# Five edits to a two-layer transformer kernel: a gate's transpose placed later, 384-column halves in two places, a scaling tied to another instruction, and probabilities times values for two key blocks in a row

## The chip, the cores and the metric

The kernel runs on one core of a Trainium2 chip, in one launch. The metric is the device time of that launch in microseconds (us); the time before is the median of three runs. The profile shows one execution. Its engines: PE is TensorE (PEld its weight loads), DVE is VectorE, ACT is ScalarE, POOL is GpSimd, SP is SyncE, which issues the DMAs here. All arrays are fp32, or fp32r where a matmul reads the high or the low part of a split number.

## The reference

Two layers of width 1024 over 512 latent tokens and 256 context tokens. Layer 0 has windowed grouped-query attention (16 heads of 64, 2 key heads, windows of three 128-blocks plus the context, a sink logit per head), layer 1 differential attention (8 heads with two score maps each). Each is followed by a squared-ReLU MLP of width 4096; a conditioning vector gives six modulation vectors per layer (`mod_x`), two of them gates.

```python
for i in range(DEPTH):
    mod_x = silu(c) @ w_ada[i] + b_ada[i]
    sh1, sc1, g1, sh2, sc2, g2 = split(mod_x)
    hx = x * (1 + sc1) + sh1
    ax = window_gqa(hx, hc, ...) if i % 2 == 0 else diff_attention(hx, hc, ...)
    x = layer_norm(alpha * x + g1 * ax, ln1_g[i], ln1_b[i])
    fx = square(relu((x * (1 + sc2) + sh2) @ mlp_w1[i])) @ mlp_w2[i]
    x = layer_norm(alpha * x + g2 * fx, ln2_g[i], ln2_b[i])
    # in layer 0 the context tokens go the same way, with their own modulation
```

In window_gqa, for a block of 128 queries: `p = softmax_with_sink(s)`, `o = p[:, lat] @ v + p[:, ctx] @ vc`.

## The kernel before

PE's instructions stand in an order that the program itself plans: `Flow` is a small simulation with jobs (generators) of given priorities; a job yields a condition, and the first job whose condition holds goes on and appends its matmuls. Costs such as `mm(n)`, `dve(n)` and `act(n)` are the planner's. The other engines and the DMA queue are ordered by the framework's scheduler; each engine then works in its order.

Every large product is made of three matmuls (`mm3`, L318 to L320): high x high, high x low, low x high. A weight tile of 128x1024 comes by DMA (w_raw), is rounded by ACT to w_h (`wsplit`), and DVE subtracts for w_l; the DMAs stand in SP's queue at L275.

Layer 0, attention (`group`, L957): 24 jobs, one for each of 6 token blocks and 4 groups of four heads. Scores go to s_ps (L977, L981), DVE and ACT make the probabilities e, then for each key block in turn four PE transposes fill pT_ps (L1028), ACT or DVE in turn copies it to pT, and `av` multiplies by the values into o_ps (L1014; one call gives four records of 128x256, in two column halves). Token blocks 0 to 5 have 4, 5, 5, 4, 2 and 2 key blocks. `pend` holds blocks whose transposes are out; a block's product is put in as soon as its own copy is done by the planner's time.

Layer 0, MLP (`mlp`, L641): four chunks of 1024 hidden units, each an up projection of 8 weight tiles over all 768 tokens (h_ps, tokens as columns in two parts, 512 and 256), squared ReLU (`post`), and a down projection of twelve groups (y_ps, weights as columns). In chunk 0 two of the tiles go in pieces of 256 columns, which leaves 30 tiles in two parts. Beside chunk 0 and later ones, the rows of the modulation (`ada_rows`, products with w_adaT on DVE into mods) are worked off as a filler. When the rows of (0, 5), the gate of this MLP, are complete, `ada_gate` starts at priority 0: `to_rows` has PE transpose mods into gate_t (L435), ACT copy it to gate_s, and a DMA write gate_d (L441). `g2` reads it at chunk 2.

Layer 1, attention: per head `proj1` makes qkv_ps for six token blocks, `post1` splits and ropes them (sk, sq, vt) and transposes to kT_ps (L1229) and qT_ps; `scores1` makes 8 score tiles per head of 128x768 in s_ps (L1324: 512 and 256 columns), whose minimum DVE takes and whose exponential ACT; `att1` transposes and multiplies. Beside it `resid1` computes the scaled residual in 16 pieces on POOL, each released (`behind`) by a kT transpose of heads 1 to 4 and blocks 0 to 3; for every four pieces it loads a part of the layer norm's gain and bias (rs_g, rs_b), which DVE scales by ALPHA (the operation is recorded at L260).

Of the kernel before, what the change touches and what calls it, by code (L numbers as in the profile page):

```python
# [19 lines left out]
P = 128  # L20
# [214 lines left out]
def hybrid_block(ctx: ExitStack, tc: tile.TileContext, t: dict, out: bass.AP):  # L235
# [27 lines left out]
    def ac(n, deps, fn, lat=LAT, **kw):  # L263
        fn(**kw)  # L264
        return fl.op("A", act(n), deps, lat)
# [176 lines left out]

    def ada_gate(l, m, dep):
        gd = dram.tile([2 - l, KT, P], F32, name=f"gate_d{l}{m}")
        yield from to_rows(mods[l][:, m] if l == 0 else mods[l][:, m, :, 0], gd, dep)
        gate_d[(l, m)] = gd.rearrange("s k p -> s (k p)")

# [193 lines left out]
    def mlp(l, hx, ready, apool, pool, ntok, acc, gates, done, extra, res, XR=0):  # L641
        ntb = ntok // P
        first = [slice(i, i + 256) for i in range(0, ntok, 256)]
        parts = [slice(0, 512)] + ([slice(512, ntok)] if ntok > 512 else [])
        fx = [pool.tile([P, D], F32, name="fx", tag="fx", bufs=ntb) for _ in range(ntb)]


# [16 lines left out]

        row_gates = gates
        for ch in range(4):
            hid = [apool.tile([P, 2, 2, ntok], F32R, name="hid", tag="A", bufs=4) for _ in range(4)]
            state = {}

            def post(ft, pt, slot, p):  # L670
                hd, fi = hid[ft // 2], ft % 2
                r = pool.tile([P, max(ntok, XR)], F32, name="relu", tag="xr", bufs=2)
                a = ac(ntok, [p], nc.scalar.activation, out=r[:, :ntok], in_=pt[:, :ntok], func=AF.Relu)
                if slot is not None:
                    sS.give(slot, a)
                if ch:
                    a = gp(pool2(ntok), [a], nc.gpsimd.tensor_tensor, out=r[:, :ntok], in0=r[:, :ntok],
                           in1=r[:, :ntok], op=ALU.mult)
                else:
                    a = dv(ntok, [a], nc.vector.tensor_tensor, out=r[:, :ntok], in0=r[:, :ntok], in1=r[:, :ntok],  # L680
                           op=ALU.mult)
                split(ntok, a, r[:, :ntok], hd[:, fi, 0], hd[:, fi, 1])
# [3 lines left out]
            for n, (ft, sl) in enumerate(order):  # L686
# [11 lines left out]
                yield w.t  # L698
                for k in range(KT):
                    c_ = slice(k * P, (k + 1) * P)  # L700
                    mm3(pt[:, sl], w.h[:, c_], w.l[:, c_], hxs(hx, k, 0, sl), hxs(hx, k, 1, sl), k == 0, k == KT - 1)
                    if k % 4 == 3:
                        p = fl.pe(12 * mm(sl.stop - sl.start))
                        if k == 3:
                            yield
# [21 lines left out]
    with tc.tile_pool(name="qpool", bufs=6, side="right") as qpool, \  # L727
# [229 lines left out]
        def group(n, tb, qd):  # L957
# [60 lines left out]
                return p  # L1018


            i = 0
            while i < len(kbs) or pend:
                yield lambda: (YES if (i < len(kbs) and fl.ok([sm_.ok, pS.ok])) or (pend and fl.ok(pend[0][3])) else NO)
                if i < len(kbs) and fl.ok([sm_.ok, pS.ok]) and len(pend) < 4:
                    pp = psm("pT_ps")
                    slot = sm_.take()
# [12 lines left out]
                    pend.append((i, kbs[i], pt_, r, xi))  # L1039
                    i += 1  # L1040
                else:
                    p = av(*pend.pop(0))
            st0["done"] += 1
            if st0["done"] % 4 == 0:
                eS.free += [p] * (1 if st0["done"] == 4 else 2)
# [132 lines left out]
    with tc.tile_pool(name="attn1", bufs=1, reuse_waits="tile") as pool:  # L1178
# [104 lines left out]
        def resid1():  # L1283
            def load(n):
                i, tb = n // NXB, n % NXB
                c = slice(i * 256, i * 256 + 256)
                if tb == 0:
                    gb[:] = [pool.tile([P, 256], F32, name="rs_" + n_, tag="rs_" + n_, bufs=1) for n_ in "gb"]
                    for k in range(2):
                        dma(256, [], out=gb[k], in_=lnrow[0, 2 + k:3 + k][:, c].broadcast_to([P, 256]))  # L1290
                        dv(128, [], nc.vector.tensor_scalar, out=gb[k], in0=gb[k], scalar1=ALPHA, scalar2=None,
                           op0=ALU.mult)
                x = pool.tile([P, 256], F32, name="rs_x", tag="rs_x", bufs=3)
                return x, dma(256, [], out=x, in_=x_spill[tb][:, c]), x_res[tb][:, c], list(gb)

# [2 lines left out]
            for n in range(4 * NXB):  # L1298
                after = yield
                x, q, dst, (g, b) = nxt  # L1300
                d = gp(pool2(256), [q], behind(nc.gpsimd.tensor_tensor, after), out=x, in0=x, in1=g, op=ALU.mult)
                d = gp(pool2(256), [d], nc.gpsimd.tensor_tensor, out=x, in0=x, in1=b, op=ALU.add)
                if old:
# [8 lines left out]
        def scores1(hd_, R):  # L1312
            kS, qTt = R["kS"], R["qT"]
            yield lambda: R["ready"]
            for qb in range(4):
                em = []
                for tt in range(2):
# [1 line left out]
                    ei = eS1.take()  # L1319
                    sp = psS("s_ps")  # L1320
                    slot = sS.take()
                    for c0, c1 in ((0, 512), (512, TOK)):
                        for hl in range(2):
                            nc.tensor.matmul(out=sp[:, c0:c1], lhsT=qTt[:, tt, hl, qb * P:(qb + 1) * P],  # L1324
                                             rhs=kS[:, tt, c0:c1], start=(hl == 0), stop=(hl == 1))
                    p = fl.pe(2 * mm(512) + 2 * mm(256))
                    nm = small.tile([P, 1], F32, name="nm", tag="nm")
                    d = dv(TOK, [p], nc.vector.tensor_reduce, out=nm, in_=sp[:, 0:TOK], axis=AX.X, op=ALU.min)
                    e = pool.tile([P, TOK], F32, name="e1", tag="e", bufs=EB1)
                    if tt == 0:  # L1330
                        sm = st["s0"][hd_ // NG][:, qb, hd_ % NG:hd_ % NG + 1]
                    else:
                        sm = small.tile([P, 1], F32, name="sm", tag="sm")
                    a = ac(TOK + 200, [d], nc.scalar.activation, out=e, in_=sp[:, 0:TOK], func=AF.Exp, scale=-1.0,
                           bias=nm, accum_out=sm)
                    sS.give(slot, a)
                    em.append((e, sm, ei, a))
                    yield
# [290 lines left out]
```

## Time and profile before

| | |
|---|---|
| median of three runs | 1710.75 us (1710.18 to 1711.88) |
| the profiled execution, its own time | 1715.99 us |
| its span, first to last instruction | 1714.2 us |
| mean granted clock of PE | 0.985 |
| PE busy | 1634.3 us, 95% |
| DVE, ACT, POOL busy | 957.7, 658.1, 345.9 us |

The profile's times are from one execution and count from its first instruction. A matmul's record ends with its last result, so consecutive ones overlap, and the distance of their starts is what one costs. The granted clock of a stretch is a share of 2.4 GHz; 0.5 is 1.2 GHz, and the two levels are the only ones seen.

### The profile page before, as it was taken

What the parts mean: (1) busy time and instruction counts of PE and PEld (TensorE: products, weight loads), DVE (VectorE), ACT (ScalarE), POOL (GpSimd) and SP (SyncE); (2) the same over time, 40 slices, a digit from 0 to 9 for tenths busy, and PEclk for the clock granted to TensorE, in tenths of its full rate; (3) what the DMA queues carried; (4) which work ended last, traced back from release to release, by engine and by line L of the source; (5) the groups of instructions that cost most, each with busy time, mean ns of one, the idle gap of its engine ahead of it and who ended that gap; (6) DMA issues with size and microseconds to landing.
All of it is one profiled execution on the core that took longest, in us unless ns stands there. A gap on an engine that the chain in (4) does not pass through costs nothing.

```text
span 1714.2 us, 23438 instructions
## 1 busy us (share of the span) xinstructions
PE 1634.3 (95%) x9129; PEld 1359.1 (79%) x9129; DVE 957.7 (56%) x1811; ACT 658.1 (38%) x1281; POOL 345.9 (20%) x314
## 2 busy tenths in 40 slices
PE   6899899999899999999999999999989799999998
PEld 4787567788778878878878998999877788888886
DVE  3665677676764644445346767777655553233336
ACT  3455555462212302302315555555542533223230
POOL 1233444200001201243220122220100001103422
PEclk9999999999999999999999999999999899999999
DMA  9110441243443434324222222211132214232321
GB/s 361 40 50 32 148 171 52 84 169 112 159 147 111 148 111 141 111 91 156 81 81 102 63 68 66 72 44 37 47 111 99 99 62 134 74 121 76 111 86 50
DMA packets 57240, 174.78 MB, mean 102 GB/s; under 512 B 7144, under 2 KB 13096, under 8 KB 57128
## 3 DMA queue, kind: packets, MB, share of 16 engines
q1 hardware_dynamic: 57128, 173.27, 29.9%
q8 instruction: 72, 1.18, 0.3%
q14 instruction: 40, 0.33, 0.1%
HBM read 165.35 MB, written 7.90 MB: 101 GB/s over the span
## 4 chain that ended last, share of the span: by engine, by line
PE 75%; DVE 9%; issue 5%; ACT 4%; POOL 3%; DMA 3%; SPq 0%; POOLq 0%; DVEq 0%; ACTq 0%
PE y_ps L320 10%; PE y_ps L319 10%; PE y_ps L318 10%; PE h_ps L318 8%; PE h_ps L319 8%; PE h_ps L320 8%; PE o_ps L1014 2%; PE qkv_ps L318 2%; PE s_ps L1324 2%; PE qkv_ps L319 2%; PE qkv_ps L320 2%; DVE e L260 2%; DVE w_l L260 2%; PE pT_ps L1028 2%; ACT w_h L264 1%
## 5 line engine op out<-in xcount | busy, mean ns | idle before, releaser
L264 ACT CAST w_h<-w_raw 128x1024 fp32r<-128x1024 f32 (+1 forms) x185 | 186.5, 1014 | 425.5 <-PE y_ps L320 214.1
L260 DVE TENSOR_TENSOR w_l<-w_raw,w_h 128x1024 fp32r<-128x1024 f32 (+1 forms) x185 | 221.9, 1209 | 223.5 <-ACT w_h L264 223.4
L319 PE MATMUL y_ps<-w_l,hid 128*128 128x512 f32 x640 | 253.0, 395 | 2.2 <-DVE w_l L260 2.2
L320 PE MATMUL y_ps<-w_h,hid 128*128 128x512 f32 x640 | 252.9, 395 | 0.6 <-DVE hid L260 0.6
L318 PE MATMUL y_ps<-w_h,hid 128*128 128x512 f32 x640 | 253.0, 395 | 0.0
L268 POOL TENSOR_TENSOR relu<-relu 128x768 f32<-128x768 f32 (+1 forms) x48 | 81.5, 1697 | 613.9 <-ACT relu L264 613.9
L320 PE MATMUL h_ps<-hx0m,w_l 128*128 128x256 f32 (+1 forms) x528 | 176.2, 334 | 0.9 <-DVE w_l L260 0.9
L318 PE MATMUL h_ps<-hx0m,w_h 128*128 128x256 f32 (+1 forms) x528 | 176.7, 335 | 0.0
L319 PE MATMUL h_ps<-hx0m,w_h 128*128 128x256 f32 (+1 forms) x528 | 176.0, 333 | 0.0
L319 PEld LDWEIGHTS y_ps<-w_l,hid 128*128 128x128 f32 x640 | 120.4, 188 | 31.7 <-DVE w_l L260 3.9
L320 PEld LDWEIGHTS y_ps<-w_h,hid 128*128 128x128 f32 x640 | 120.4, 188 | 30.1 <-DVE hid L260 1.9
L318 PEld LDWEIGHTS y_ps<-w_h,hid 128*128 128x128 f32 x640 | 120.4, 188 | 28.4
L318 PE MATMUL qkv_ps<-w_h,hx 128*128 128x384 f32 (+1 forms) x384 | 128.2, 334 | 0.2
L319 PE MATMUL qkv_ps<-w_l,hx 128*128 128x384 f32 (+1 forms) x384 | 123.7, 322 | 0.8 <-DVE w_l L260 0.8
L320 PE MATMUL qkv_ps<-w_h,hx 128*128 128x384 f32 (+1 forms) x384 | 123.4, 321 | 0.0
L268 POOL TENSOR_TENSOR e<-e,sm 128x512 f32<-128x512 f32 (+2 forms) x96 | 95.4, 1010 | 127.6 <-DVE sm L260 107.1
L318 PE MATMUL h_ps<-hx1m,w_h 128*128 128x512 f32 (+1 forms) x288 | 108.1, 375 | 3.5 <-ACT relu L264 3.5
L320 PEld LDWEIGHTS h_ps<-hx0m,w_l 128*128 128x128 f32 x528 | 99.7, 189 | 12.9 <-DVE w_l L260 1.7
L318 PEld LDWEIGHTS h_ps<-hx0m,w_h 128*128 128x128 f32 x528 | 99.7, 189 | 11.4 <-ACT w_h L264 0.2
L319 PEld LDWEIGHTS h_ps<-hx0m,w_h 128*128 128x128 f32 x528 | 99.7, 189 | 11.3
L319 PE MATMUL h_ps<-hx1m,w_h 128*128 128x512 f32 (+1 forms) x288 | 107.6, 374 | 0.0
L320 PE MATMUL h_ps<-hx1m,w_l 128*128 128x512 f32 (+1 forms) x288 | 107.5, 373 | 0.0
(225 smaller groups left out, 3124.1 us busy)
## 6 DMA issues: line engine op xcount, KB each, us to landing
w_raw<-in_w SPq DMA_DIRECT2D x128, 512.0 KB, 3.5
w_raw<-in_w_adaT SPq DMA_DIRECT2D x56, 512.0 KB, 3.5
w_raw<-in_w_ada SPq DMA_DIRECT2D x24, 512.0 KB, 3.9
w_raw<-in_b_w SPq DMA_DIRECT2D x32, 384.0 KB, 3.4
raw<-in_w_ada SPq DMA_DIRECT2D x16, 512.0 KB, 9.6
w_raw<-in_a_wq SPq DMA_DIRECT2D x8, 512.0 KB, 7.1
w_raw<-in_a_wo SPq DMA_DIRECT2D x8, 512.0 KB, 3.6
w_raw<-in_b_wo SPq DMA_DIRECT2D x8, 512.0 KB, 4.4
```

What stands on the lines that cost most here:

```text
L260: fn(**kw)
L264: fn(**kw)
L268: fn(**kw)
L318: nc.tensor.matmul(out=o, lhsT=lh, rhs=rh, start=start, stop=False)
L319: nc.tensor.matmul(out=o, lhsT=lh, rhs=rl, start=False, stop=False)
L320: last["pe"] = nc.tensor.matmul(out=o, lhsT=ll, rhs=rh, start=False, stop=stop)
L1014: nc.tensor.matmul(out=po[odd * HD:odd * HD + HD, 0:256], lhsT=vv[:, kb, kvh], rhs=pt_[:, odd * 256:odd * 256 + 256], start=(i == 0), stop ...
L1028: nc.tensor.transpose(out=pp[:, c * P:(c + 1) * P], in_=es[j][:, i * P:(i + 1) * P], identity=ident)
L1324: nc.tensor.matmul(out=sp[:, c0:c1], lhsT=qTt[:, tt, hl, qb * P:(qb + 1) * P], rhs=kS[:, tt, c0:c1], start=(hl == 0), stop=(hl == 1))
```

## The change

- `ada_gate`: for gate (0, 5), the job first waits until chunk 1 of layer 0's MLP begins (`st2["second"]`).
- `mlp`: with 768 tokens the two parts are 384 and 384; the second part's results start at column 512 of the PSUM tile, and ReLU reads both through a view of two pieces.
- `group`: the product is put into PE's order when two blocks' copies are done, or the last one is left alone; both products follow each other without another job between.
- `resid1`: the scaling of rs_g and rs_b moves from the load to the first of the four pieces, tied to the same kT transpose.
- `scores1`: two parts of 384 columns, at columns 0 and 512; the minimum and the exponential go over the view of two pieces.

```diff
--- before.py
+++ after.py
@@ -442,6 +442,8 @@
 
     def ada_gate(l, m, dep):
         gd = dram.tile([2 - l, KT, P], F32, name=f"gate_d{l}{m}")
+        if (l, m) == (0, 5):
+            yield lambda: YES if "second" in st2 else NO
         yield from to_rows(mods[l][:, m] if l == 0 else mods[l][:, m, :, 0], gd, dep)
         gate_d[(l, m)] = gd.rearrange("s k p -> s (k p)")
 
@@ -641,7 +643,8 @@
     def mlp(l, hx, ready, apool, pool, ntok, acc, gates, done, extra, res, XR=0):
         ntb = ntok // P
         first = [slice(i, i + 256) for i in range(0, ntok, 256)]
-        parts = [slice(0, 512)] + ([slice(512, ntok)] if ntok > 512 else [])
+
+        parts = [slice(0, 512)] if ntok <= 512 else [slice(0, ntok // 2), slice(ntok // 2, ntok)]
         fx = [pool.tile([P, D], F32, name="fx", tag="fx", bufs=ntb) for _ in range(ntb)]
 
 
@@ -664,13 +667,19 @@
 
         row_gates = gates
         for ch in range(4):
+            if l == 0 and ch == 1:
+                st2["second"] = True
             hid = [apool.tile([P, 2, 2, ntok], F32R, name="hid", tag="A", bufs=4) for _ in range(4)]
             state = {}
 
             def post(ft, pt, slot, p):
                 hd, fi = hid[ft // 2], ft % 2
                 r = pool.tile([P, max(ntok, XR)], F32, name="relu", tag="xr", bufs=2)
-                a = ac(ntok, [p], nc.scalar.activation, out=r[:, :ntok], in_=pt[:, :ntok], func=AF.Relu)
+                ro, ri = r[:, :ntok], pt[:, :ntok]
+                if ntok > 512 and ft >= n0:
+                    ro = ro.rearrange("p (b t) -> p b t", b=2)
+                    ri = pt.rearrange("p (b t) -> p b t", b=2)[:, :, 0:ntok // 2]
+                a = ac(ntok, [p], nc.scalar.activation, out=ro, in_=ri, func=AF.Relu)
                 if slot is not None:
                     sS.give(slot, a)
                 if ch:
@@ -698,7 +707,8 @@
                 yield w.t
                 for k in range(KT):
                     c_ = slice(k * P, (k + 1) * P)
-                    mm3(pt[:, sl], w.h[:, c_], w.l[:, c_], hxs(hx, k, 0, sl), hxs(hx, k, 1, sl), k == 0, k == KT - 1)
+                    po = sl if ft < n0 or sl.start == 0 else slice(512, 512 + sl.stop - sl.start)
+                    mm3(pt[:, po], w.h[:, c_], w.l[:, c_], hxs(hx, k, 0, sl), hxs(hx, k, 1, sl), k == 0, k == KT - 1)
                     if k % 4 == 3:
                         p = fl.pe(12 * mm(sl.stop - sl.start))
                         if k == 3:
@@ -1018,9 +1028,13 @@
                 return p
 
 
+            def av_ok():
+                return (len(pend) > 1 or len(pend) == 1 and i == len(kbs)) and fl.ok([x[3] for x in pend[:2]])
+
+
             i = 0
             while i < len(kbs) or pend:
-                yield lambda: (YES if (i < len(kbs) and fl.ok([sm_.ok, pS.ok])) or (pend and fl.ok(pend[0][3])) else NO)
+                yield lambda: (YES if (i < len(kbs) and fl.ok([sm_.ok, pS.ok])) or av_ok() else NO)
                 if i < len(kbs) and fl.ok([sm_.ok, pS.ok]) and len(pend) < 4:
                     pp = psm("pT_ps")
                     slot = sm_.take()
@@ -1039,7 +1053,8 @@
                     pend.append((i, kbs[i], pt_, r, xi))
                     i += 1
                 else:
-                    p = av(*pend.pop(0))
+                    for _ in range(min(2, len(pend))):
+                        p = av(*pend.pop(0))
             st0["done"] += 1
             if st0["done"] % 4 == 0:
                 eS.free += [p] * (1 if st0["done"] == 4 else 2)
@@ -1288,8 +1303,6 @@
                     gb[:] = [pool.tile([P, 256], F32, name="rs_" + n_, tag="rs_" + n_, bufs=1) for n_ in "gb"]
                     for k in range(2):
                         dma(256, [], out=gb[k], in_=lnrow[0, 2 + k:3 + k][:, c].broadcast_to([P, 256]))
-                        dv(128, [], nc.vector.tensor_scalar, out=gb[k], in0=gb[k], scalar1=ALPHA, scalar2=None,
-                           op0=ALU.mult)
                 x = pool.tile([P, 256], F32, name="rs_x", tag="rs_x", bufs=3)
                 return x, dma(256, [], out=x, in_=x_spill[tb][:, c]), x_res[tb][:, c], list(gb)
 
@@ -1298,6 +1311,9 @@
             for n in range(4 * NXB):
                 after = yield
                 x, q, dst, (g, b) = nxt
+                for y in (g, b) if n % NXB == 0 else ():
+                    dv(128, [], behind(nc.vector.tensor_scalar, after), out=y, in0=y, scalar1=ALPHA, scalar2=None,
+                       op0=ALU.mult)
                 d = gp(pool2(256), [q], behind(nc.gpsimd.tensor_tensor, after), out=x, in0=x, in1=g, op=ALU.mult)
                 d = gp(pool2(256), [d], nc.gpsimd.tensor_tensor, out=x, in0=x, in1=b, op=ALU.add)
                 if old:
@@ -1319,20 +1335,21 @@
                     ei = eS1.take()
                     sp = psS("s_ps")
                     slot = sS.take()
-                    for c0, c1 in ((0, 512), (512, TOK)):
+                    for c in range(2):
                         for hl in range(2):
-                            nc.tensor.matmul(out=sp[:, c0:c1], lhsT=qTt[:, tt, hl, qb * P:(qb + 1) * P],
-                                             rhs=kS[:, tt, c0:c1], start=(hl == 0), stop=(hl == 1))
-                    p = fl.pe(2 * mm(512) + 2 * mm(256))
+                            nc.tensor.matmul(out=sp[:, c * 512:c * 512 + 384], lhsT=qTt[:, tt, hl, qb * P:(qb + 1) * P],
+                                             rhs=kS[:, tt, c * 384:c * 384 + 384], start=(hl == 0), stop=(hl == 1))
+                    sv = sp.rearrange("p (b t) -> p b t", b=2)[:, :, 0:384]
+                    p = fl.pe(4 * mm(384))
                     nm = small.tile([P, 1], F32, name="nm", tag="nm")
-                    d = dv(TOK, [p], nc.vector.tensor_reduce, out=nm, in_=sp[:, 0:TOK], axis=AX.X, op=ALU.min)
+                    d = dv(TOK, [p], nc.vector.tensor_reduce, out=nm, in_=sv, axis=AX.XY, op=ALU.min)
                     e = pool.tile([P, TOK], F32, name="e1", tag="e", bufs=EB1)
                     if tt == 0:
                         sm = st["s0"][hd_ // NG][:, qb, hd_ % NG:hd_ % NG + 1]
                     else:
                         sm = small.tile([P, 1], F32, name="sm", tag="sm")
-                    a = ac(TOK + 200, [d], nc.scalar.activation, out=e, in_=sp[:, 0:TOK], func=AF.Exp, scale=-1.0,
-                           bias=nm, accum_out=sm)
+                    a = ac(TOK + 200, [d], nc.scalar.activation, out=e.rearrange("p (b t) -> p b t", b=2),
+                           in_=sv, func=AF.Exp, scale=-1.0, bias=nm, accum_out=sm)
                     sS.give(slot, a)
                     em.append((e, sm, ei, a))
                     yield
```

## Rows read from the trace of the kernel before

**Rows 1.** The page, chain that ended last, share of the span by engine.

```profile
PE 75%; DVE 9%; issue 5%; ACT 4%; POOL 3%; DMA 3%; SPq 0%; POOLq 0%; DVEq 0%; ACTq 0%
```

**Rows 2.** PE timeline: start us, us, engine, line, operation, count, [idle <-ender].

```profile
428.78 0.28 PE L320 MATMUL h_ps<-hx0m,w_l 128*128 128x256 f32 x1
433.91 0.38 PE L435 MATMUL gate_t<-identr,mods 128*16 128x128 f32 x1 [4.85 <-DVE mods L260]
```

**Rows 3.** DVE timeline, the write of mods.

```profile
433.69 0.17 DVE L260 TENSOR_TENSOR mods<-mods,c_badaT 128x16 f32<-128x16 f32 x1
```

**Rows 4.** Stretches: us; PE, PEld, DVE, ACT, POOL busy; PEclk, DMA share, GB/s.

```profile
434.00:438.80 4.80, 4.80 (x12) 3.77 (x12) 3.46 (x5) 1.30 (x2) 0.00 (x0) 0.50 0.63 211
1001.60:1005.40 3.80, 3.79 (x18) 3.80 (x19) 2.76 (x4) 1.56 (x4) 0.00 (x0) 0.55 0.64 205
60.00:250.00 190.00, 179.68 (x1288) 134.18 (x1288) 120.37 (x345) 101.50 (x215) 73.35 (x66) 1.00 0.25 86
```

**Rows 5.** PE timeline, an earlier weight tile of chunk 0.

```profile
411.85 0.50 PE L320 MATMUL h_ps<-hx0m,w_l 128*128 128x512 f32 x1 [0.53 <-DVE w_l L260]
```

**Rows 6.** ACT timeline, start of chunk 1.

```profile
522.42 1.05 ACT L264 CAST w_h<-w_raw 128x1024 fp32r<-128x1024 f32 x1 [1.09 <-DMA w_raw<-in_w]
```

**Rows 7.** DVE timeline, layer 1's attention, second pair of scalings.

```profile
999.56 0.29 DVE L260 TENSOR_SCALAR rs_g<-rs_g 128x256 f32<-128x256 f32 x1 [1.60 <-DMA rs_g<-in_lnrow]
...
1000.97 0.29 DVE L260 TENSOR_SCALAR rs_b<-rs_b 128x256 f32<-128x256 f32 x1 [0.92 <-DMA rs_b<-in_lnrow]
```

**Rows 8.** PE timeline, holes at the second and third pair, and at 1128.

```profile
1001.61 0.33 PE L1229 MATMUL kT_ps<-identr,sk 128*128 128x128 f32 x2 [2.31 <-DVE sk L260]
...
1042.88 0.30 PE L1434 MATMUL rmsT<-identr,rms_sb 128*128 128x128 f32 x1 [0.93 <-ACT w_h L264]
1043.96 0.33 PE L1229 MATMUL kT_ps<-identr,sk 128*128 128x128 f32 x2 [0.78 <-DVE rr L260]
...
1046.32 0.60 PE L1449 MATMUL rmsB<-identr,rr 128*2 128x128 f32 x4 [0.54 <-POOL rr L268]
...
1128.88 0.38 PE L1449 MATMUL rmsB<-identr,rr 128*2 128x128 f32 x2 [1.03 <-POOL rr L268]
```

**Rows 9.** PE timeline, a later head's weight.

```profile
1093.59 0.44 PE L319 MATMUL qkv_ps<-w_l,hx 128*128 128x384 f32 x1 [0.56 <-DVE w_l L260]
```

**Rows 10.** PE timeline, first matmul of each group of 24 and of the next.

```profile
562.59 0.39 PE L318 MATMUL h_ps<-hx0m,w_h 128*128 128x512 f32 x1
...
568.18 0.28 PE L318 MATMUL h_ps<-hx0m,w_h 128*128 128x256 f32 x1
...
571.01 0.39 PE L318 MATMUL h_ps<-hx0m,w_h 128*128 128x512 f32 x1
...
1052.82 0.33 PE L318 MATMUL qkv_ps<-w_h,hx 128*128 128x384 f32 x1
...
1056.99 0.40 PE L1324 MATMUL s_ps<-kS,qT 128*128 128x512 f32 x1
```

**Rows 11.** DVE groups by form: count | busy us, mean ns | idle before.

```profile
L260 DVE CUSTOM_DVE_ANT_0 e<-s_ps,mask,nsink 128x512 f32<-128x512 f32 x16 | 11.7, 742 | 1.5 <-PE s_ps L981 1.5
L260 DVE CUSTOM_DVE_ANT_1 e<-s_ps,mask,nsink 128x512 f32<-128x512 f32 x16 | 11.6, 742 | 1.0 <-PE s_ps L981 0.9
```

**Rows 12.** PE timeline, layer 0's attention; last, L1014's waits (us, times).

```profile
102.84 1.25 PE L1028 MATMUL pT_ps<-identr,e 128*128 128x128 f32 x10
104.02 0.65 PE L1014 MATMUL o_ps<-pT,v 128*64 128x256 f32 x4
104.60 0.66 PE L1028 MATMUL pT_ps<-identr,e 128*128 128x128 f32 x4
105.19 1.08 PE L1014 MATMUL o_ps<-pT,v 128*64 128x256 f32 x8
106.21 0.50 PE L977 MATMUL s_ps<-kT,qT 128*128 128x256 f32 x2
...
  ACT pT L264: 4.8, 8
```

## The prediction

> **What bounds the kernel now.** I read the page first: TensorE (PE) is busy for most of the span, and the chain that ended last is 75% PE [rows 1]. PE's instruction stream is nearly the whole time, so an edit is worth something only where it closes a hole in that stream, shortens it, or lifts the clock. Hence three further views: the PE timeline, where a hole stands in brackets with the one who ended it; the timelines of VectorE (DVE) and ScalarE (ACT) around each hole; and the table by stretches for the granted clock. The profiled execution took 1715.99 us, 5.2 us over the 1710.75 us median; I work out differences in its rows and subtract them from the median.
>
> **The change part by part.** Five edits.
>
> *Gate (0,5).* The transpose at L435 stands in PE's order after the matmul of 428.78 and runs at 433.91: 4.85 us idle until DVE has written mods [rows 2]. DVE writes it at 433.69, behind other work [rows 3]. Nothing reads this gate before chunk 2; the edit puts the transpose at the start of chunk 1, a whole down projection later, when mods is long there. Removed: 433.91 - 428.78 less one matmul of 0.12, so 5.0 us. Behind the hole, 434.0 to 438.8 runs at a granted 0.50, the lower level, 1.2 GHz [rows 4]; at 2.4 GHz that work takes half, 2.4 us more. Late next is the weight's low part, w_l, which does not hang on the gate: a tile shortly before waited 0.53 us for it [rows 5]. I give back 0.5 us for each of the two tiles that follow. All that the step issues moves with it: the transpose (its row says 0.38 us, part of it under the next matmul [rows 2]); ACT's copy of 16x128, which fits into the 1.09 us that ACT waits there for a weight's DMA [rows 6]; and the gate_d DMA, now among SyncE's (SP's) loads of chunk 1's weights. For the last there is no row at the new place; a load behind it comes later by at most that same 1.09 us, and I take zero, because PE works 8.4 us on a weight tile [rows 10] and the loads run a tile ahead. Without that cover it is 1.1 us. Net -6.4 us (bounds -2.9, if the clock returns nothing and the load is late, to -7.4).
>
> *Scaling of the layer-0 gains in layer 1's attention.* The two DVE scalings follow their loads, and DVE stands for the DMA: 1.60 us before 999.56 and 0.92 us before 1000.97 [rows 7]. sk comes behind them in DVE's order, and PE waits 2.31 us for it [rows 8]; 1001.6 to 1005.4 then runs at a granted 0.55 [rows 4], so 3.8 x 0.45 = 1.7 us are lost to the clock. At 1041 the next pair stands before rms_sb and sk, and PE has holes of 0.93, 0.78 and 0.54 us; the same place two heads on, without a pair, has 1.03 us [rows 8]: 1.2 us. I found no hole of PE behind the other two of the four pairs. The eight scalings stay (0.29 us each [rows 7]), but wait for PE's kT transpose of the next head, when the DMA has landed. Returned: without the hole the next head wants its last weight sooner; behind the third pair, where PE did not stop, such a w_l cost 0.56 us and slower starts around it [rows 9], so I give back 1.0. The edit adds a wait on DVE for PE. Queued behind it are vt, rope and sk of the next token blocks and w_l, for which PE's next kT and projections wait; POOL's rs_x products, behind the same kT today, get the scaling before them. Four places, bounded by zero and 1.6 us each (the standing they replace), 0.1 taken inside the 1.0. Net 2.3 + 1.7 + 1.2 - 1.0 = -4.2 us (bounds -5.2 and +1.2, if all 6.4 of the four come back).
>
> *Layer 0's MLP in 384 + 384 columns instead of 512 + 256.* 30 weight tiles, each with 24 matmuls of either size; their number stays. A 512 group goes from 562.59 to 568.18 = 5.59 us, a 256 group to 571.01 = 2.83, and 24 of 384 in layer 1 from 1052.82 to 1056.99 = 4.17 [rows 10]. 8.42 - 8.34 = 0.08 us, times 30 = 2.4 us. But a straight line through 256 and 512 gives zero, and in those 384s the tokens are the stationary operand; I take the middle, -1.2 us (0 to -2.4). The Trainium skill, "TensorE: Matmul & The Clock Gate", section "Back-to-back issue gap", has N/2.4 + 2.5 ns for a matmul of N columns, by which both splits are equal and this term is 0; for a stream with weight loads it states 131 ns at 512 columns, where the trace has 5.59 / 24 = 233 ns, and the measurement decides. ReLU now reads two pieces of 384: DVE's masked read of 512 score columns takes 742 ns as one piece and 742 ns as pieces [rows 11], so nothing.
>
> *Layer 1's scores in 384 + 384.* 64 tiles of four matmuls, weights unchanged: by the same groups 2 x 233 + 2 x 118 - 4 x 174 = 6 ns a tile, 0.4 us at most; I take -0.2. The minimum and the exponential over two pieces: nothing, as above.
>
> *Two key blocks in a row.* One block's product is four records. Alone it holds PE from 104.02 to 104.60 (0.58 us), two in a row from 105.19 to 106.21 (1.02 us); the four transposes between take 0.59 us, while ten in a row take 1.18, so four would take 0.47 [rows 12]. A merge saves 2 x 0.58 - 1.02 + 0.12 = 0.26 us. Going through L1014's rows, I count 88 blocks in 48 runs: 19 of one, 23 of two, one of three, five of four (the first of one and of two stand in [rows 12]). The new rule makes two, three, three, two, one and one calls for the six token blocks, 48 over four head groups, so the count falls only where a run now splits as 1-2-1 or 1-1. I found two and three of these: 5 merges, -1.3 us. But the order of the whole stage is planned anew. From 60 to 250 PE is busy 179.7 of 190 us [rows 4]; two fifths of those 10.3 us, 4 us, is my bound for what the new order may lose or win.
>
> Sum: 6.4 + 4.2 + 1.2 + 0.2 + 1.3 = 13.3 us; 1710.75 - 13.3 = **1697.4 us**.
>
> **The rivals.**
> - *Layer 1 swaps one wait for another*: DVE waits for kT, the weights are late, 0 instead of 4.2. 1701.6 us. For: DVE has 2.76 us of work in the 3.8 us behind the hole [rows 4], so it has little to give. Against: what it stands for today is a DMA, 2.5 us in one go [rows 7].
> - *The holes close, the clock does not follow*, its low stretches come elsewhere: 2.4 + 1.7 less, 1701.5 us. For: other holes remain. Against: these two low stretches stand right behind the two holes [rows 2, 4, 8].
> - *The last edit doesn't do what it says*, runs stay at 48: 1698.7 us, inside the range.
> - *Longer rows of transposes pull the clock down.* Waiting for two blocks puts eight transposes where four stood. A new low stretch like the two of [rows 4] costs 1.7 us or more; six of 1.7 take back 10.2: 1707.6 us. Against: ten in a row at 102.84 [rows 12], and 60 to 250 ran at a granted 1.00 throughout [rows 4]. The same page of the Trainium skill, section "Part 4: PE-mode transpose", says that transposes don't count as busy for the clock in the same way, which is this mechanism; these rows do not bear it out.
> - *Slower: PE waits for the second copy.* A pair can't start before both pT copies are done, and where one product covered the next one's copy PE may now stand. Price: eight products waited 4.8 us for ACT's pT [rows 12], 0.6 us each; if all 48 calls did, 28.8 us against the 13.3: 1726.2 us. It decides from (13.3 + 3.4) / 48 = 0.35 us a call. Against: while a pair isn't ready, projections and scores are put into PE's order instead.
>
> **How the numbers follow.** Forecast 0.66, layer 1 swaps 0.14, no merges 0.07, clock 0.06, transposes 0.04, second copy 0.03. The low end adds the far bounds, 7.4 + 5.2 + 2.4 + 0.4 + 1.3 + 4 = 20.7: 1690. The high end takes in both 1701s and most of the 4 us of a new order: 1705. What can be told from no change is 0.2%, 3.4 us: the forecast and the first three rivals are faster by more, transposes give about the same, and a bad order on top of a rival eats into both. Faster 0.91, same 0.05, slower 0.04.
>
> **What would show it.** No hole before gate_t, which stands at the start of chunk 1, and a granted 1.00 where 434 to 439 was; no rs_g row on DVE with an idle time ended by a DMA, and kT without its 2.31 us; h_ps groups of 24 matmuls of 384 in 4.17 to 4.21 us; some 43 runs of o_ps in layer 0, none of one block but each fifth. Wrong would be: holes before o_ps ended by pT, holes of DVE ended by kT with sk late behind them, or low-clock stretches where there are none today.

## The result

| | before | after |
|---|---|---|
| median of five runs | 1710.75 us (1709.49 to 1711.88) | 1697.34 us (1693.66 to 1701.68) |
| ratio of the times, 95% interval | 1 | 0.9922 [0.9901, 0.9942] |
| the profiled execution, its own time; its span | 1715.99; 1714.2 | 1701.68; 1699.9 |
| mean granted clock of PE | 0.985 | 0.988 |
| PE busy | 1634.3 us | 1626.4 us |

13.4 us faster, as forecast to 0.1 us. The experiments show that this closeness is luck, errors that cancel: of the five terms the gate's is about right, the scaling's and, timed together, the two for columns show nothing, and the one for two key blocks is five times too small.

The page of the changed kernel, the chain that ended last ([rows 1] before):

```profile
PE 75%; DVE 10%; issue 5%; ACT 5%; DMA 3%; POOL 3%; SPq 0%; DVEq 0%; POOLq 0%; ACTq 0%
```

PE is busy for 1626.4 of the 1699.9 us, so its stream is still nearly the whole time, and the stages tell where the time went. Windows of the kernel before, then of the changed one: layer 0's attention up to its first xn_t; chunk 0's up projection; layer 1's attention up to its last scores (columns: the stretch, its length, busy time and instructions of PE, PEld, DVE, ACT, POOL; granted clock, DMA share, GB/s):

```profile
78.81:352.63 273.82, 261.58 (x1739) 193.97 (x1738) 179.22 (x546) 136.21 (x310) 103.34 (x104) 0.99 0.28 96
373.62:453.08 79.46, 71.87 (x444) 63.48 (x443) 54.23 (x83) 29.90 (x53) 0.55 (x1) 0.96 0.41 138
933.55:1274.39 340.84, 323.09 (x2171) 301.21 (x2170) 240.11 (x514) 192.17 (x456) 60.96 (x75) 0.98 0.19 61
```

```profile
78.29:346.10 267.81, 256.79 (x1738) 193.48 (x1737) 180.62 (x548) 135.75 (x310) 102.25 (x104) 0.99 0.31 99
367.09:442.36 75.27, 70.97 (x444) 69.20 (x442) 51.99 (x81) 29.75 (x52) 0.55 (x1) 0.98 0.40 132
922.72:1263.59 340.87, 324.36 (x2171) 306.95 (x2170) 241.53 (x514) 191.96 (x456) 61.80 (x75) 0.98 0.19 61
```

Layer 0's attention, where 1.3 us were forecast, is 6.0 us shorter; chunk 0, 4.2; layer 1's attention, where 4.4 were forecast (scaling and scores), has not moved: 340.84 and 340.87. The remaining 3.5 us between the two profiles lie behind the last of these windows, in code that no edit touches, in low-clock stretches at other places. That is a reading trap: the profiled execution of before was, with 1715.99 us, slower than all other runs of that kernel (at most 1714.38), so a difference of two profiles is not yet a difference of two kernels.

The gate. PE timeline: a wait for w_l in chunk 0 of the kernel before, the tile after that of [rows 5]; then, in the changed kernel, the four waits for w_l in chunk 0 and the transpose at its new place ([rows 2] before):

```profile
420.84 0.50 PE L320 MATMUL h_ps<-hx0m,w_l 128*128 128x512 f32 x1 [0.34 <-DVE w_l L260]
```

```profile
407.34 0.44 PE L320 MATMUL h_ps<-hx0m,w_l 128*128 128x384 f32 x1 [0.64 <-DVE w_l L260]
...
416.38 0.44 PE L320 MATMUL h_ps<-hx0m,w_l 128*128 128x384 f32 x1 [0.45 <-DVE w_l L260]
...
425.32 0.45 PE L320 MATMUL h_ps<-hx0m,w_l 128*128 128x384 f32 x1 [0.35 <-DVE w_l L260]
...
434.27 0.45 PE L320 MATMUL h_ps<-hx0m,w_l 128*128 128x384 f32 x1 [0.21 <-DVE w_l L260]
...
509.81 0.28 PE L435 MATMUL gate_t<-identr,mods 128*16 128x128 f32 x1
```

The hole of 4.85 us is gone, the transpose waits for nothing, and w_l is late next, as the prediction had it. But it was late for two tiles before, too, by 0.53 [rows 5] and 0.34 us: of the 1.65 us in four waits 0.8 are new. Layer 0's products ([rows 12] before), same view:

```profile
102.09 1.93 PE L1042 MATMUL pT_ps<-identr,e 128*128 128x128 f32 x16
...
103.96 1.08 PE L1024 MATMUL o_ps<-pT,v 128*64 128x256 f32 x8
```

Pairs, as the edit says. But layer 1 has a new hole, where the kernel before had none over 0.3 us, and the window behind it shows the clock at its lower level:

```profile
1061.32 0.34 PE L1244 MATMUL kT_ps<-identr,sk 128*128 128x128 f32 x2 [1.70 <-DVE sk L260]
...
1065.30 0.88 PE L1406 MATMUL pT_ps<-identr,e 128*128 128x128 f32 x4 [0.60 <-DVE pT L260]
```

```profile
1062.40:1065.80 3.40, 2.80 (x14) 2.30 (x13) 1.90 (x5) 1.44 (x3) 0.81 (x2) 0.50 0.27 77
```

### The profile page after: what moved, and what is told of

Same layout as the page of the kernel before. It is cut to its first block, busy times and chain, and to the rows that moved or that the text cites. A ratio compares the mean times of both kernels' runs of the same rounds, so it can differ in the third digit from the quotient of the medians.

```text
span 1699.9 us, 23452 instructions
## 1 busy us (share of the span) xinstructions
PE 1626.4 (96%) x9129; PEld 1394.2 (82%) x9129; DVE 955.2 (56%) x1811; ACT 657.8 (39%) x1281; POOL 346.6 (20%) x314
## 4 chain that ended last, share of the span: by engine, by line
PE 75%; DVE 10%; issue 5%; ACT 5%; DMA 3%; POOL 3%; SPq 0%; DVEq 0%; POOLq 0%; ACTq 0%
PE y_ps L320 10%; PE y_ps L319 10%; PE y_ps L318 10%; PE h_ps L318 8%; PE h_ps L319 8%; PE h_ps L320 8%; PE qkv_ps L318 2%; PE qkv_ps L319 2%; PE qkv_ps L320 2%; PE s_ps L1340 2%; PE o_ps L1024 2%; DVE w_l L260 2%; DVE e L260 2%; PE pT_ps L1042 2%; PE o_ps L1378 1%
## 5 line engine op out<-in xcount | busy, mean ns | idle before, releaser
L260 DVE TENSOR_TENSOR w_l<-w_raw,w_h 128x1024 fp32r<-128x1024 f32 (+1 forms) x185 | 221.8, 1210 | 220.1 <-ACT w_h L264 219.2
L320 PE MATMUL h_ps<-hx0m,w_l 128*128 128x384 f32 (+1 forms) x528 | 176.2, 334 | 1.6 <-DVE w_l L260 1.6
L318 PE MATMUL h_ps<-hx0m,w_h 128*128 128x384 f32 (+1 forms) x528 | 176.3, 334 | 0.2 <-ACT w_h L264 0.2
L319 PE MATMUL h_ps<-hx0m,w_h 128*128 128x384 f32 (+1 forms) x528 | 175.8, 333 | 0.0
```

The lines of the kernel that those rows point to most:

```text
L318: nc.tensor.matmul(out=o, lhsT=lh, rhs=rh, start=start, stop=False)
L319: nc.tensor.matmul(out=o, lhsT=lh, rhs=rl, start=False, stop=False)
L320: last["pe"] = nc.tensor.matmul(out=o, lhsT=ll, rhs=rh, start=False, stop=stop)
```

## The experiments

Each kernel was timed beside the kernel before on the same chip:

| kernel | median us | before, beside it | ratio [95%] |
|---|---|---|---|
| e1 gate alone | 1705.48 | 1711.19 | 0.9968 [0.9956, 0.9981] |
| e2 scaling alone | 1710.78 | 1711.19 | 1.0000 [0.9990, 1.0010] |
| e3 columns alone | 1709.86 | 1711.19 | 1.0001 [0.9989, 1.0013] |
| e4 two blocks alone | 1703.89 | 1711.19 | 0.9963 [0.9950, 0.9975] |
| e5 all but two blocks | 1702.28 | 1710.18 | 0.9955 [0.9940, 0.9970] |
| e6 rule for the first four jobs | 1710.02 | 1710.18 | 1.0003 [0.9991, 1.0015] |
| e7 rule for the last eight jobs | 1710.09 | 1710.18 | 0.9996 [0.9983, 1.0010] |
| e8 all but scaling | 1698.75 | 1710.18 | 0.9934 [0.9919, 0.9948] |
| e9 scaling on POOL | 1708.91 | 1708.97 | 0.9994 [0.9985, 1.0003] |
| e10 changed, scaling on POOL | 1696.41 | 1708.97 | 0.9929 [0.9916, 0.9942] |
| e11 gate and two blocks | 1699.70 | 1708.97 | 0.9942 [0.9929, 0.9954] |
| e12 filler kept for the end | 1708.34 | 1710.51 | 0.9990 [0.9980, 1.0000] |

An amount in us below is 1710 times the distance of the ratio from 1. Diffs are against the kernel before unless said otherwise.

**e1, the gate alone.** The hunk of `ada_gate` and the line that sets `st2["second"]`.

> The kernel before with the gate edit alone. Theory P (the prediction's terms): the hole of 4.85 us before gate_t and the low clock behind it go, about 1 us comes back as waits for w_l; -6.4 us, 1704.4. Theory Q (the clock only moves on, as a new low stretch at 372.9 to 376.3 in the changed kernel's profile suggests): the hole goes, a low stretch of 3.4 us stands elsewhere in chunk 0; -4 to -5 us. In both the first weight matmul of chunk 1's down projection comes as much earlier as the whole.

5.5 us faster (3.2 to 7.5): the term of 6.4 lies within that interval, and so do the 4 to 5 us of theory Q. The stage shows both. Chunk 0 takes 78.4 to 79.7 us in the eight profiles with the gate's old place, and 72.5 to 73.4 in four of the six with the new one, 6.3 us less. In the other two (after and e11, 75.3 and 75.0) a low-clock stretch of 3.4 us stands near its start, behind a hole at xn_t, and takes back some 2 us, as theory Q had it. Over all six the stage is 5.6 us shorter.

**e2, the scaling alone.** The two hunks of `resid1`.

> The kernel before with the scaling of layer 1's gains tied to the kT transpose, alone. Theory P: -4.2 us, 1706.5, the holes of 2.31 us at the second pair and of 1.2 us at the third gone. Theory R (swapped waits; in the changed kernel's profile layer 1's attention, first projection to last score, is as long as before): no change, 0 to -1 us, new holes before kT of about the same sum.

Nothing (1.7 us slower to 1.7 faster), where 4.2 us were forecast: theory R, swapped waits. The holes of 2.31, 0.93 and 0.78 us [rows 8] are gone, and none of the eight scalings waits for its DMA any more [rows 7] or for anything else. But PE has a hole of 1.70 us at 1072.74 with 3.4 us at a granted 0.50 behind it, and shorter new ones: 0.39 us at 990 and 0.60 at 1076 for copies to pT, 0.55 for a w_l at 1006; rmsB's 0.54 us at 1046 are 1.03 at 1042.

```profile
1043.04 0.60 PE L1450 MATMUL rmsB<-identr,rr 128*2 128x128 f32 x4 [1.03 <-POOL rr L268]
...
1072.74 0.34 PE L1229 MATMUL kT_ps<-identr,sk 128*128 128x128 f32 x2 [1.70 <-DVE sk L260]
...
1076.84 0.43 PE L1390 MATMUL pT_ps<-identr,e 128*128 128x128 f32 x1 [0.60 <-DVE pT L260]
```

VectorE's timeline ahead of the hole of 1.70 us, in this kernel and then at the same place in the kernel before:

```profile
1070.10 0.69 DVE L260 SCALAR_TENSOR_TENSOR nl<-s,nlam,rc 128x1 f32<-128x1 f32 x1
1070.83 1.56 DVE L260 SCALAR_TENSOR_TENSOR e<-e,nl,e 128x768 f32<-128x768 f32 x1
1072.31 0.28 DVE L260 TENSOR_TENSOR sk<-rope,sk 128x128 fp32r<-128x128 f32 x1
```

```profile
1073.65 0.22 DVE L260 SCALAR_TENSOR_TENSOR nl<-s,nlam,rc 128x1 f32<-128x1 f32 x1
1073.78 0.29 DVE L260 TENSOR_TENSOR sk<-rope,sk 128x128 fp32r<-128x128 f32 x1
1073.99 1.50 DVE L260 SCALAR_TENSOR_TENSOR e<-e,nl,e 128x768 f32<-128x768 f32 x1
```

The same three instructions, but the 1.56 us multiplication of e now stands ahead of sk, for which PE's kT waits. With the eight scalings of 0.29 us some twenty of the stage's 505 other VectorE instructions changed places in the order that the scheduler wrote; with the scaling back at its old place in the changed kernel (e8) that order is, by tiles and shapes, the one of before. Over all profiles the stage's length goes from 337.7 to 342.3 us with the low-clock stretches that fall into it (6.8 to 17.1 us of them), not with the edit: 338.8 to 341.2 in the five with it (e2, e5, e9, e10, after).

**e3, the columns alone.** The hunks of `mlp` for the parts, and `scores1`.

> The kernel before with 384 + 384 columns in layer 0's MLP and layer 1's scores, alone. Theory P: -1.4 us (0 to -2.8), 1709.3; 24 matmuls of 384 columns from MLP tokens in 4.17 to 4.21 us start to start. Rival: time is proportional to columns and nothing changes.

Nothing (2.2 us slower to 1.9 faster). The reads in two pieces cost nothing: ReLU takes 808 ns before and 806 in e3, the exponential 905 and 906, the minimum 952 and 952. The trace shows where the gain stays: a chunk of 384-column matmuls comes in two speeds. First matmul of successive groups of 24, changed kernel, in chunk 1 (two lines) and in chunk 2 (two lines):

```profile
514.09 0.34 PE L318 MATMUL h_ps<-hx0m,w_h 128*128 128x384 f32 x1
...
518.25 0.34 PE L318 MATMUL h_ps<-hx0m,w_h 128*128 128x384 f32 x1
...
648.19 0.34 PE L318 MATMUL h_ps<-hx0m,w_h 128*128 128x384 f32 x1
...
652.43 0.34 PE L318 MATMUL h_ps<-hx0m,w_h 128*128 128x384 f32 x1
```

4.16 and 4.24 us, and each of the chunks 1 to 3 keeps its speed from its second group to its end. A chunk of 8 tiles takes 66.6 us at the one and 67.84 at the other, with 512 + 256 always 67.2 to 67.3. In e3 chunks 1 and 3 were slow and 2 fast; in the changed kernel and e10 1 fast, 2 and 3 slow; in e5 and e8 1 and 2 fast, 3 slow: seven fast and eight slow. A fast tile gains 0.08 us, a slow one loses 0.07, so over the stage they about cancel. What decides the speed of a chunk isn't known.

**e4, two key blocks in a row alone.** The two hunks of `group`.

> The kernel before with two key blocks in a row, alone. Theory P: five merges of 0.26 us, -1.3 us, 1709.4, the stage's new order plus or minus 4. Theory S (from the changed kernel's profile, where the product's runs number 47 instead of 48, yet the attention of layer 0 ends 6.5 us sooner): the gain is the new order, fewer holes and a low-clock stretch less; -5 to -6.5 us, with 46 to 48 runs.

6.3 us faster (4.3 to 8.6): the 5 to 6.5 of theory S, not the 1.3 of theory P. Runs of o_ps number 47 against 48, and one run less is worth 0.26 us at the prediction's price, so merging did not pay for it. PE's waits in the stage, kernel before and then this one (us in total, times, longest):

```profile
PE s_ps L977 <- DVE nm L260: 3.9, 5, 1.1
PE ada_t L384 <- ACT ada_rows L264: 2.1, 2, 1.3
PE ada_ps L360 <- DMA w_raw<-in_w_ada: 2.0, 2, 1.0
PE o_ps L1014 <- ACT pT L264: 1.7, 2, 1.4
PE pT_ps L1028 <- POOL e L268: 1.7, 1, 1.7
```

```profile
PE s_ps L977 <- DVE nm L260: 4.6, 8, 1.6
PE o_ps L1014 <- ACT pT L264: 2.2, 2, 1.4
PE ada_t L384 <- ACT ada_rows L264: 1.6, 1, 1.6
PE o_ps L1014 <- DVE pT L260: 1.5, 1, 1.5
PE ada_ps L360 <- DMA w_raw<-in_w_ada: 1.0, 1, 1.0
```

The waits are much the same, 11.4 and 10.9 us; products wait 2 us more for their copies, and the wait for POOL's e is gone. That one stood at the end of the stage, before:

```profile
321.39 1.35 PE L1014 MATMUL o_ps<-pT,v 128*64 128x256 f32 x8
322.67 0.33 PE L1028 MATMUL pT_ps<-identr,e 128*128 128x128 f32 x1
324.66 1.34 PE L1028 MATMUL pT_ps<-identr,e 128*128 128x128 f32 x7 [1.67 <-POOL e L268]
326.24 1.97 PE L1014 MATMUL o_ps<-pT,v 128*64 128x256 f32 x8 [0.24 <-ACT pT L264]
328.14 0.80 PE L318 MATMUL y_ps<-w_h,hx 128*128 128x512 f32 x1
```

```profile
326.20:329.50 3.30, 3.26 (x11) 1.88 (x12) 0.95 (x2) 0.37 (x1) 0.00 (x0) 0.50 0.00 0
```

The last job's transposes have nothing beside them, and eight records of o_ps take 1.97 us where 1.08 are usual: the clock is at its lower level from 326.1 on for 3.4 us. In e4's order six matmuls of the output projection (y_ps) stand between each of the last transposes and products:

```profile
318.16 1.03 PE L1032 MATMUL pT_ps<-identr,e 128*128 128x128 f32 x8
...
320.51 1.08 PE L1014 MATMUL o_ps<-pT,v 128*64 128x256 f32 x8
```

So the next theory was E: the gain is this end, and the pairs are incidental.

**e5, all but two blocks.** The changed kernel without the hunks of `group`.

> The four other edits together, without the two key blocks in a row. Theory S (the last edit is worth 6 to 7 us, the gate 5 to 6, scaling and columns nothing, as they measured alone): 5 to 6.5 us below the kernel before, ratio 0.9962 to 0.9971, and layer 0's attention ends where it ended before. The prediction's sum (13.3 less 1.3): 12.0 us below, ratio 0.9930.

7.7 us faster (5.1 to 10.3): the sum of the terms measured alone, 5.3, is just inside that interval, the prediction's 12.0 outside. Layer 0's attention takes 273.5 us, as before.

**e6 and e7, the rule for some of the jobs.** Against the two hunks of `group`, where `av_ok` and the loop fall back to one block (in e7 `n >= 16` stands for `n < 4`):

```diff
             def av_ok():
+                if not (n < 4):
+                    return pend and fl.ok(pend[0][3])
...
-                    for _ in range(min(2, len(pend))):
+                    for _ in range(min(2, len(pend)) if n < 4 else 1):
```

> Kernel before with the new rule for the first four jobs only (token block 0). PE's order then has 52 runs of o_ps, 22 of them of one block, against 48 and 19 before, but the last o_ps of the stage have output-projection matmuls between them, as in the changed kernel. Theory E (the gain of the last edit is the hole of 1.67 us and the low clock behind it at the end of the stage, 322 to 330 us of the kernel before, not the pairing): 4 to 6 us below the kernel before, ratio 0.9965 to 0.9977. Theory P (pairs pay, by 0.26 us a merged run): four runs more, 1.0 us above, ratio 1.0006.

> Kernel before with the new rule for the last eight jobs only (token blocks 4 and 5). PE's order has 45 runs of o_ps, three fewer than before, and the end of the stage is ordered as before: transposes of the last job with no other matmul to run beside them. Theory E: the hole near 323 us and the low clock behind it stay, 0 to 0.8 us below the kernel before (three merges by 0.26), ratio 0.9995 to 1.0. Theory P, if the 6.5 us of the whole edit belong to the pairs: a share by key blocks, 16 of 88, 1.2 us, and the hole matters nothing, ratio 0.9993; a gain of 4 us or more here would refute E.

Neither shows a gain: e6 is 0.5 us slower (2.6 slower to 1.5 faster), e7 0.7 faster (1.7 slower to 2.9 faster). In e7 there are three runs fewer, at 45, and the end keeps its hole (POOL's e: 1.7 us). The 4 us that would refute E are excluded; whether three merges pay 0.8 us or nothing can't be told. But e6 breaks E in its strong form: its end is closed, and the scores wait elsewhere instead, 7.1 us for nm against 3.9 before:

```profile
PE s_ps L977 <- DVE nm L260: 3.7, 8, 1.2
PE s_ps L981 <- DVE nm L260: 3.4, 3, 1.8
```

**e12, the end alone.** To part the end from the pairs without redoing the order ahead of it:

```diff
-                yield lambda: odone[tb] if len(odone[tb]) == 4 else NO
+                yield lambda: odone[tb] if len(odone[tb]) == 4 and (tb != 4 or st0["done"] >= 22) else NO
```

> Kernel before with one condition more in the output projection: the 24 matmuls of token block 4 wait until 22 of the 24 attention jobs are done. PE's order is that of the kernel before up to the last dozen groups of the stage; runs of o_ps stay at 48, with the same lengths, and the four groups of six output-projection matmuls now stand between the last transposes and products, where the kernel before had the hole of 1.67 us. Theory E (what the last edit gained is this end): 3.5 to 5 us below the kernel before, ratio 0.9971 to 0.998. Theory N (the stage only moves its holes: without those matmuls the scores before them wait for the minimum, as with the rule for four jobs): 0 to 1 us, ratio 0.9994 to 1.0, with more time in s_ps ended by nm.

1.7 us faster (0 to 3.4): the interval holds the 0 to 1 of theory N and ends just short of the 3.5 to 5 of theory E. PE's timeline at the end, with y_ps groups in between again:

```profile
323.30 0.60 PE L1028 MATMUL pT_ps<-identr,e 128*128 128x128 f32 x4
...
326.01 0.65 PE L1014 MATMUL o_ps<-pT,v 128*64 128x256 f32 x4
```

The wait for POOL's e is gone, and so is the low clock at 326; nm takes back 0.8 us at 311 to 313, where the y_ps groups had stood. By the middle of this run, and by the stage's length, the end is worth some 2 us, a third of the edit, but nothing is not excluded.

The stage in all profiles, split into PE's holes, the low clock at half its length, and the rest, which is the matmul stream at 2.4 GHz with its changes of shape (worked out from PE's timeline, one profile for each kernel; the ends of PE's records are modelled, so the holes are better as differences than as lengths):

| order of layer 0's attention | length | holes | at 1.2 GHz | rest |
|---|---|---|---|---|
| as before (before, e1, e2, e3, e5, e9) | 272.4 to 274.9, mean 273.6 | 12.2 | 5.7 | 258.5 (258.2 to 258.7) |
| two blocks (e4, e8, e10, e11, after) | 266.3 to 267.8, mean 267.0 | 11.3 | 0.7 | 255.4 (255.1 to 255.6) |
| e6 | 274.9 | 13.5 | 3.4 | 259.7 |
| e7 | 270.8 | 12.6 | 0 | 258.2 |
| e12 | 271.7 | 11.3 | 3.4 | 258.8 |

The 6.5 us of the edit are 0.9 of holes, 2.5 of clock and 3.1 of stream. The stream is the surprise, and the number of runs, 47 for 48, does not explain it; what stands beside the transposes explains a part. In the order of before 27 rows of transposes go straight into o_ps, and 18 runs of o_ps straight into transposes; with pairs it is 22 and 12, because while a job waits for its second copy, scores and projections are put between. A transpose followed by o_ps holds PE 0.21 us, followed by a score 0.03; the first transpose behind o_ps takes 0.17 where others take 0.11. From one start to the next, without waits, all transposes of pT_ps cost 42.7 us before and 40.7 in e4, and those of ada_t 4.6 and 3.6. The two prices explain 1.3 of the 2.0 (5 x 0.18 + 6 x 0.06), and the two transposes stretched beside the end's hole 0.4; the rest of the 3.1, some 1.4, I can't assign. e7, where the neighbours are as before (27 and 18), has the stream of before within 0.3.

**e8, all but scaling,** and **e11, gate and two blocks** (no scaling, no columns):

> The changed kernel with the scaling where it was before. Theory R (layer 1's attention only swaps one set of holes for another): 12 to 14.5 us below the kernel before, ratio 0.9915 to 0.993, as the changed kernel's 0.9922; the holes of 2.31, 0.93 and 0.78 us are back, that of 1.70 us is gone. The prediction's term (4.2 us): 9.2 us below, ratio 0.9946.

> Only the gate and the two key blocks in a row. If scaling and columns are worth nothing, as alone: 11.5 to 13.5 us below the kernel before, ratio 0.992 to 0.9933, as the changed kernel and as all but scaling. By the prediction's terms for these two (6.4 + 1.3): 7.7 us, ratio 0.9955.

11.3 us (8.9 to 13.9) and 9.9 us (7.9 to 12.1), beside 13.3 (9.9 to 16.9) for all five edits: the two edits that show a gain alone carry the change, and both intervals hold the 11.8 that they sum to. The prediction's 7.7 for e11 lies just below its interval; its 9.2 for e8 just inside. In e8 the first three holes of layer 1 are back (2.21, 0.94 and 0.86 us) and that of 1.70 is gone. Whether scaling and columns add the 1 to 3 us between these kernels can't be told from these runs.

**e9 and e10, the scaling by POOL,** alone and in the changed kernel, to take VectorE out of it. The diff is against the changed kernel; e9 has the same new lines in the kernel before:

```diff
-                    dv(128, [], behind(nc.vector.tensor_scalar, after), out=y, in0=y, scalar1=ALPHA, scalar2=None,
+                    gp(pool2(256) / 2, [], behind(nc.gpsimd.tensor_scalar, after), out=y, in0=y, scalar1=ALPHA, scalar2=None,
                        op0=ALU.mult)
```

> Kernel before with the scaling moved as in the change, tied to the same kT transpose, but done by POOL instead of DVE. DVE then neither waits for the DMA nor has the scalings in its order, and its sk stand ahead of the multiplication of e as in the kernel before. Theory D (the change's scaling gained nothing because DVE's order was redone and an sk came behind a multiplication of e of 1.56 us): the holes of 2.31, 0.93 and 0.78 us go and none of 1.70 us comes; 3 to 4.5 us below the kernel before, ratio 0.9974 to 0.9982. Theory R (layer 1's attention turns whatever is taken out there into later waits for weights): 0 to 1 us, ratio 0.9994 to 1.0.

> The changed kernel with the same scaling by POOL. Theory D: 3 to 4.5 us below the changed kernel, that is 16 to 18 us below the kernel before, ratio 0.9895 to 0.9906. Theory R: as the changed kernel, ratio 0.992 to 0.9934.

Theory D falls: e9 is 1.0 us faster (0.5 slower to 2.6 faster), and e10 is the changed kernel's time. The order of sk and e is before's again, and the trace shows the holes gone. kT's waits in layer 1's attention, in the kernel before, then e2, then e9 (total, times, longest; the longest that stays in e2 and e9 is a hole of 2.32 us near 1210, which all three kernels have):

```profile
PE kT_ps L1229 <- DVE sk L260: 8.5, 6, 2.3
```

```profile
PE kT_ps L1229 <- DVE sk L260: 7.8, 6, 2.3
```

```profile
PE kT_ps L1229 <- DVE sk L260: 6.2, 5, 2.3
...
PE qkv_ps L319 <- DVE w_l L260: 1.3, 3, 0.6
```

Holes in the stage add up to 17.7 us before, 17.0 in e2 and 15.6 in e9. Of the 2.1 us that e9 gains there, the stream at full clock takes back 1.4 (318.1 us against 316.7; 318.2 in e10). So even with both the DMA and VectorE out of the way the term is 0.7 us by the stage and 1.0 by the runs, not 4.2. What stretches the stream under POOL's scalings wasn't followed up.

## Why the prediction was right, and where it was not

- *Gate*: forecast 6.4, measured 5.5 (3.2 to 7.5). The hole, the clock behind it and w_l as next in line are all in the trace. The give-back of 2 x 0.5 us was too large, since two of the waits were there before: 1.65 us less 0.87, 0.8 in the changed kernel, and 1.20 less 0.87, 0.3 in e1. What came instead, in two of six profiles, is a low-clock stretch near the chunk's start, 1.7 us, which the second rival had foreseen.
- *Scaling*: forecast 4.2, measured 0. The step that failed is the price of the new order on VectorE, "0.1 taken inside the 1.0", though its bound of 6.4 had all of it coming back. It priced the moved instructions' own waits, and the moved scalings wait for nothing; what came was that others (sk and e) changed places. That is a part of the cause only: with the order of before kept, in e9, it is still no more than 1.0, and why the stream is longer there stays open. It also counted 1.7 us for a low-clock stretch. Behind the old hole (1.9 to 2.35 us) that stretch is there in eight of nine profiles, but taking the hole away doesn't save it: one stands behind the new hole in two of three, and the stage has 12.8 us at the lower level in the mean of the five profiles with the scaling moved, 10.9 in the nine without. The zero is what the first rival gave, at 0.14, but not by its mechanism: VectorE doesn't wait for kT ahead of the scalings, and one w_l is late anew, by 0.55 us.
- *Columns*: forecast 1.4, measured -0.2. The far bound, 0.08 us a tile, is real in every fast chunk; that 384 has a second speed the prediction's row, one group of layer 1 at 4.17 us, could not show.
- *Two blocks*: forecast 1.3, measured 6.3 (4.3 to 8.6), at its middle beyond the 4 us given as a bound for a new order. Two steps failed. The bound was read from PE's idle time between 60 and 250 us [rows 4], at a granted 1.00; the stage goes on to 352, and there stood the hole for POOL's e and both low-clock stretches, and the stream, which gave half of the gain, was in no bound beyond the merges. And the count of runs, 48 less 5, left out that the rule also splits: there were 19 runs of one block, 23 of two, one of three and five of four, and now there are 7, 39, one and none. Twelve single blocks made six pairs, but the five runs of four made ten, so 47 are left. The price of 0.26 us a run is neither shown nor refuted: e6 has four runs more and 1.2 us more of stream, e7 three fewer and 0.3 less.
- *Rivals*: the second copy costs 1 to 2 us in all (2.2 + 0.6 us of o_ps behind pT after, 3.7 in e4, 1.7 before), not 0.6 a call; other work stands in between, as the prediction's "against" said. The 0.6 was a misreading, too: the view behind "4.8, 8" [rows 12] adds the idle time of the weight loads (PEld) to PE's own, and PE's products waited for ACT's pT twice, 1.7 us in all. Sixteen transposes in a row (102.09) drew no low clock. Of the signs of being wrong that the prediction named one is there: low-clock stretches at 372.9 and at 1062.4 us, at places where the kernel before has none.
- *Sum*: 13.3 forecast, 13.4 seen, with 4.2 + 1.6 too much and 5.0 too little in it. The terms as timed alone add up to 11.6; the gate's 0.9 and the 1.8 that are left are inside the intervals. That the sum came out to 0.1 us is luck.

## What to carry to other kernels

A change that alters an order written by a planner or scheduler is worth what its new order is worth, and that is not read from the instructions it moves: look through the whole stage for holes that other work could fill, its end above all, and at which shapes follow each other on PE. Bound such a term over the whole stage, and give it the width that it has. When a sum comes out right, time its terms one by one before believing them.

## What the runs showed of the hardware

- A matmul of 384 columns (fp32r, 128 rows, new weights each) ran in one of two steady rhythms, 4.16 or 4.24 us for 24, one of them through a whole chunk of layer 0's MLP and not the same from chunk to chunk, in the same program text and at a granted 1.00.
- Low-clock stretches move between executions of the same order on PE: behind the hole of 1.67 us at the end of layer 0's attention there was one in all six profiles with that order, but at 254 us in four of the six, and in e7 a hole of 1.66 us at the same place had none behind it. A forecast can count the hole; the clock behind it only as likely.
- On PE the matmul of 128x64 (o_ps) is dear to enter and to leave: 0.31 us from its last record to the next of any other shape, and 0.21 from a transpose or a score into it, where a transpose to the next takes 0.11.
